# Two projections of a hybrid attention block as groups of seven block products inside the last attention heads

## The chip, the cores and the metric

The kernel runs on one core of a Trainium2 chip. Times are microseconds (us) of device time of one execution. TensorE is PE, VectorE DVE, ScalarE ACT, GpSimd POOL, SyncE SP (here it only issues transfers).

## The reference, cut to what matters

```
h = rms_norm(x, norm_g)                       # x: 512 tokens x 1024, float32
proj = h @ w_in                               # 1024 x 6152
fq,fk,fv,fz, mq,mk,mv,mz, ga,gb, fl = split(proj)   # 8 x 512, 2 x 1024, 8 columns
y_fox  = fox_attention(rms(fq), rms(fk), fv, log_sigmoid(fl + b_f)) * silu(fz)
y_moba = moba_attention(rope(rms(mq)), rope(rms(mk)), mv) * silu(mz)
merged = sigmoid(ga + b0) * (y_fox @ w_fox) + sigmoid(gb + b1) * (y_moba @ w_moba)
out = x + merged @ w_out
```

Each branch has 8 heads of 64. With 512 tokens and key blocks of 256, both attentions are causal attention over 512 keys.

## The kernel before, in words

Every float32 product is made of three float32r products. `split` makes of a weight chunk (128 x 1024) a rounded part `wh` (ACT, L134) and a rest `wl` (DVE, L136); the activations are held as `Gh` and `Gl`; PE adds Gh·wh + Gh·wl + Gl·wh.

A plain projection of 256 columns (`mkb` is k of the last four MoBA heads, `mqb` their q, `mvb` their v) is 4 `unit`s of 128 tokens, each 2 x 4 x 3 matmuls of 256 columns: 96 matmuls. A group (`GZ0` is z of MoBA, both halves; `GA0`, `GA1`, `GB0`, `GB1` are the gates) computes a 2 x 2 block product with seven block products instead of eight. It needs differences of the weight blocks (DVE, `sub`) and sums of the activations, which are made early, written to DRAM (`s_dram`) and read back (`load_sums`, by POOL's queue, when the stage `gates` begins). One of the seven products is 24 matmuls of 256 columns.

Four attention stages (`plan`) of four heads each: fox a, fox b, MoBA a, MoBA b. For each pair of heads `Tr` transposes q and k (`p_qT`, `p_kT`) and writes `QS`, `KH`, `KL`; a transfer copies `KH` to the other half of the partitions. For each head `Aa` makes four logit tiles (`lg`, PE), each masked with its row maximum taken (DVE, tile `p` and `negm`, L558) and exponentiated (ACT); `Bb` transposes the probabilities (`p_a`, `p_b`, `p_cc`), splits them (`pth` on ACT, `ptl` on DVE) and multiplies by v (`pv`); the result `y` (`yma`, `ymb`) is one DVE addition, and RECIPROCAL takes the inverse row sums of a pair of heads. The transposes rotate through three PSUM tiles (`tp`).

`inter` puts work from a list (`filler`) between the steps of a stage: in MoBA a `mkb`, `mqb` and half of `mvb`, in MoBA b the rest of `mvb` and `wf0` to `wf3` (y_fox @ w_fox, 24 matmuls of 512 columns each, tile `pf`). Then come `GZ0`, `GA0` and the rest. `pump` issues loads of weight chunks (SP's queue, four buffers `wr`) and their splits up to three places ahead of the unit that is reached; with `issue_after` the splits of `wf` stand behind the last DVE instruction written so far. A scheduler then fixes the order on every engine at build time; the engines run it in that order.

Of the kernel before, what the change touches and what calls it, by code (L numbers as in the profile page):

```python
# [29 lines left out]
def fox_moba_kernel(ctx: ExitStack, tc, xT, x, w_in, w_fl, w_fox, w_moba, w_out, cst, rope, out):  # L30
# [203 lines left out]
    rbc = con.tile([P, S], F32, name="rbc")  # L234


    def norm_row():
# [450 lines left out]


    PRODUCTS = (("A11", 1), ("S3", 3), ("A12", 2), ("S2", 1), ("S1", 1), ("A22", 3), ("S4", 1))  # L690
    Z_ORDER = (0, 2, 1, 3, 5, 4, 6)
    groups = {}

    def group(name):
        ga, gz, i = name[1] == "A", name[1] == "Z", int(name[2])
        wa, wb = ("mza", "mzb") if gz else (f"g{'a' if ga else 'b'}{i}", f"g{'a' if ga else 'b'}{i + 2}")
# [12 lines left out]

        def prep(n):  # L710

            def go():
                if n == 1:
                    sub(R["11"], R["12"], R["11"])
                    sub(R["12"], R["22"], R["12"])
                elif n == 3:
                    sub(R["12"], R["22"], R["11"])
                elif n == 5:
                    sub(R["21"], R["21"], R["12"])
                key = ("11", "12", "21", "12", "11", "21", "22")[n]  # L720
# [32 lines left out]
        def add(u, half, n, b):  # L753
            V.tensor_tensor(out=u[:, :, half * HT:(half + 1) * HT], in0=two(st[b]), in1=two(st["e", n]), op=OP.add)

        def evac(n):
            if n == 0:
                if ga or i == 0 and not gz:
# [20 lines left out]
        def silu2(o, z):  # L779
            s = t2("u", 3, "sg").rearrange("p (c t) -> p c t", t=z.shape[2])  # L780
            A.activation(s, z, AF.Tanh, scale=0.5)
            V.scalar_tensor_tensor(o, s, 1.0, z, op0=OP.add, op1=OP.mult)

        def finish_z(q):
            u = st["u"][q]
            for c in range(2):
                o = u[:, :, c * HT:(c + 1) * HT] if q else u[:, c:c + 1, :]
                silu2(o, two(st[1]) if q and c == 0 else o)
            for c in range(2):
                G.tensor_tensor(out=YM[2 * q + c], in0=YM[2 * q + c], in1=u[:, c, :], op=OP.mult)  # L790

        def finish(q):
            if gz:
                return finish_z(q)
# [19 lines left out]
        groups[name] = [unit(n) for n in order_]  # L814

    def merge_a(i, c):
        if True:
# [53 lines left out]
    def group_o():  # L871
# [94 lines left out]
        def evac(n):  # L966
# [13 lines left out]
            else:  # L980
# [260 lines left out]
```

## Time and profile before

| | |
|---|---|
| three timed runs | 424.75, 424.85, 425.29 us (median 424.85) |
| the profiled execution | 424.55 us, its span 422.8 us |
| granted TensorE clock, mean | 0.998 |
| busy, share of the span | PE 98%, DVE 79%, ACT 65%, POOL 26% |

The span is the time from the first to the last record; all times below count from its start. The profiled execution lies 0.3 us under the median of the timed runs.

### The profile page before, as it was taken

Reading aid. Unit: us, or ns where it says so; the run is one execution under the profiler, and the core shown is the slowest. Engines: PE = TensorE matmul, PEld = TensorE weight load, DVE = VectorE, ACT = ScalarE, POOL = GpSimd, SP = SyncE. Lnnn points to the kernel's source line nnn. Section 1 sums busy time; section 2 is a strip of 40 time slices with the busy share of each in tenths; the row PEclk is TensorE's granted clock in tenths of the full one; section 3 lists DMA queues with packets and bytes.
Section 4 is the critical chain, followed back from the end, with each engine's and each line's share of the span. In section 5 each row is a group of like instructions: output and inputs, shape, how many; then the busy total and the mean of one; then the engine's idle time right before and its main releaser. Section 6 shows DMA issues by size and latency. Waiting matters only on the chain.

```text
span 422.8 us, 7826 instructions
## 1 busy us (share of the span) xinstructions
PE 415.2 (98%) x2956; PEld 387.7 (92%) x2956; DVE 334.5 (79%) x571; ACT 273.6 (65%) x521; POOL 109.5 (26%) x127
## 2 busy tenths in 40 slices
PE   7999999999999999999999999999999999999996
PEld 6998899999999999999988789999999989988884
DVE  4669978798889877597457769998998675788982
ACT  4985337877788767797379845666756525685550
POOL 1059300252023880417501042134000020022240
PEclk9999999999999999999999999999999999999999
DMA  7981244654264432241211039705151726796494
GB/s 246 399 314 50 60 140 137 183 165 154 50 226 120 158 101 80 71 121 32 99 34 44 28 96 373 252 13 188 39 162 52 248 51 152 243 246 108 82 159 159
DMA packets 26373, 59.52 MB, mean 141 GB/s; under 512 B 3168, under 2 KB 7968, under 8 KB 26336
## 3 DMA queue, kind: packets, MB, share of 16 engines
q1 hardware_dynamic: 13552, 38.38, 27.5%
q0 software_dynamic: 3968, 9.44, 10.4%
q10 hardware_dynamic: 8816, 11.21, 9.1%
q8 instruction: 23, 0.38, 0.4%
q14 instruction: 14, 0.11, 0.1%
HBM read 48.37 MB, written 6.32 MB: 129 GB/s over the span
## 4 chain that ended last, share of the span: by engine, by line
PE 83%; DVE 6%; DMA 5%; ACT 2%; issue 2%; SPq 1%; DVEq 0%; ACTq 0%
PE pb_GB L744 3%; PE pb_GA L744 3%; PE pb_GA L741 3%; PE pb_GB L741 3%; PE pb_GA L743 3%; PE pb_GB L743 3%; PE po L943 3%; PE po L945 3%; PE po L944 3%; PE pv L609 2%; PE pv L610 2%; PE lg L556 2%; PE lg L555 2%; PE pf L666 2%; PE pf L668 2%; DMA x<-in_x_dram 2%
## 5 line engine op out<-in xcount | busy, mean ns | idle before, releaser
L330 POOL TENSOR_TENSOR ff<-ss,mh 128x8 f32<-128x8 f32 x16 | 28.3, 1771 | 59.4 <-DVE ss L328 58.8
L560 ACT ACTIVATE p<-p,negm 128x128 f32<-128x128 f32 (+1 forms) x64 | 35.6, 557 | 8.9 <-DVE negm L558 8.6
L558 DVE CUSTOM_DVE_ANT_0 p<-lg,mask 128x128 f32<-128x128 f32 (+1 forms) x64 | 30.2, 485 | 8.3 <-PE lg L556 6.9
L134 ACT ACTIVATE wh_GB<-wr_gb 128x1024 fp32r<-128x1024 f32 x14 | 14.6, 1058 | 13.9 <-PE pm L667 5.9
L905 ACT ACTIVATE wh_o<-wr_o 128x1024 fp32r<-128x1024 f32 x14 | 14.8, 1060 | 9.7 <-PE pb_GB L743 2.8
L555 PE MATMUL lg<-KH,QS 128*128 128x128 f32 (+1 forms) x64 | 20.9, 332 | 0.0
L136 DVE TENSOR_TENSOR wl_GB<-wr_gb,wh_GB 128x1024 fp32r<-128x1024 f32 x14 | 16.8, 1220 | 5.0 <-ACT wh_GB L134 5.0
L136 DVE TENSOR_TENSOR wl_GA<-wr_ga,wh_GA 128x1024 fp32r<-128x1024 f32 x14 | 19.2, 1388 | 1.5 <-ACT wh_GA L134 1.5
L906 DVE TENSOR_TENSOR wl_o<-wr_o,wh_o 128x1024 fp32r<-128x1024 f32 x14 | 16.9, 1220 | 2.4 <-ACT wh_o L905 2.3
L134 ACT ACTIVATE wh_GA<-wr_ga 128x1024 fp32r<-128x1024 f32 x14 | 14.4, 1056 | 6.9 <-DVE wr_ga L702 3.0
L826 POOL DMA_DIRECT2D uGB<-f x4 | 3.5, 871 | 58.2 <-issue 48.2
L529 DVE SCALAR_TENSOR_TENSOR QS<-p_qT,cs,QS 64x512 fp32r<-64x512 f32 x16 | 12.0, 750 | 5.7 <-ACT QS L528 5.4
L606 DVE TENSOR_TENSOR ptl<-p_b,pth 128x512 fp32r<-128x512 f32 x16 | 11.0, 684 | 6.2 <-ACT pth L605 6.1
L528 ACT ACTIVATE QS<-p_qT,cs 64x512 fp32r<-64x512 f32 x16 | 10.9, 681 | 4.4 <-PE p_qT L519 3.0
L744 PE MATMUL pb_GA<-Gh,wl_GA 128*128 128x256 f32 x48 | 13.5, 281 | 0.0
L744 PE MATMUL pb_GB<-Gh,wl_GB 128*128 128x256 f32 x48 | 13.5, 281 | 0.0
L743 PE MATMUL pb_GA<-Gl,wh_GA 128*128 128x256 f32 x48 | 13.5, 281 | 0.0
L741 PE MATMUL pb_GA<-Gh,wh_GA 128*128 128x256 f32 x48 | 13.5, 281 | 0.0
L741 PE MATMUL pb_GB<-Gh,wh_GB 128*128 128x256 f32 x48 | 13.5, 280 | 0.0
L743 PE MATMUL pb_GB<-Gl,wh_GB 128*128 128x256 f32 x48 | 13.5, 280 | 0.0
L666 PE MATMUL pf<-yhf,wh_wf 128*128 128x512 f32 x32 | 13.0, 407 | 0.3 <-ACT f L680 0.3
L668 PE MATMUL pf<-yhf,wl_wf 128*128 128x512 f32 x32 | 12.6, 403 | 0.2 <-DVE wl_wf L136 0.2
(483 smaller groups left out, 1821.4 us busy)
## 6 DMA issues: line engine op xcount, KB each, us to landing
wr_ga<-in_w_in_dram SPq DMA_DIRECT2D x8, 512.0 KB
wr_gb<-in_w_in_dram SPq DMA_DIRECT2D x8, 512.0 KB
wr_o<-in_w_out_dram SPq DMA_DIRECT2D x8, 512.0 KB
xt<-in_xT_dram SPq DMA_DIRECT2D x8, 256.0 KB
x<-in_x_dram SPq DMA_DIRECT2D x8, 256.0 KB
KH<-KH ACTq DMA_DIRECT2D x16, 128.0 KB
s_dramh<-sum_h ACTq DMA_DIRECT2D x8, 256.0 KB
s_draml<-xt ACTq DMA_DIRECT2D x8, 256.0 KB
```

The lines of the kernel that those rows point to most:

```text
L134: A.activation(hi[:, :, 0:n], src, AF.Copy)
L136: eng.tensor_tensor(out=lo[:, q, 0:n], in0=src[:, q], in1=hi[:, q, 0:n].bitcast(F32), op=OP.subtract)
L330: G.tensor_tensor(out=f2, in0=ss.rearrange("p t h -> p (t h)"), in1=mh, op=OP.pow)
L555: T.matmul(lg[:, :n], qs[:, qt], kh[:, :n], start=True, stop=False)
L558: V.tensor_tensor_reduce(pt, lg[:, :n], mask[:, 512 - n:512], -0.125, 3.0e38, op0=OP.add, op1=OP.min, accum_out=mkn[:, hh, i:i + 1])
L560: A.activation(pt, pt, AF.Exp, bias=mkn[:, hh, i:i + 1], scale=-1.0, accum_out=rs[:, hh, i:i + 1])
L666: T.matmul(p, hi[:, k, cc], yh, start=(k == 0), stop=False)
L668: T.matmul(p, lo[:, k, cc], yh, start=False, stop=(k == 3))
L741: T.matmul(o, hi[:, k, cc], lh, start=(n < 3 and c == 0 and k == 0), stop=False, skip_group_check=True)
L743: T.matmul(o, hi[:, k, cc], ll, start=False, stop=False, skip_group_check=True)
L744: T.matmul(o, lo[:, k, cc], lh, start=False, stop=(k == 3), skip_group_check=True)
L906: V.tensor_tensor(out=wide(lo), in0=wide(R[key, c]), in1=wide(hi).bitcast(F32), op=OP.subtract)
```

## The change

`mqb` and `mkb` become one group `GQ0` of seven products (q and k side by side as two weight columns, tokens as rows): 168 matmuls in place of 192. `GZ0` moves from behind the attention into the filler of MoBA b, ahead of `wf0`; `wf1` to `wf3` move behind the attention. Both groups read their sums through small slots: `A` is the two fox tiles `Q2t` and two `sm` tiles, `B` the tile of `rbc` and three `y` tiles, `C` the second token half of `Gh` and `Gl` (free once `mvb` is done). Each slot is loaded twice by SP's queue. `load_sums` stays for the gates.

```diff
-            ("m", "a", C_MQ, C_MK, ["mkb", "mqb", "mvb:01"]),
-            ("m", "b", C_MQ, C_MK, ["mvb:23", "wf0", "wf1", "wf2", "wf3"]))
+            ("m", "a", C_MQ, C_MK, ["GQ0", "mvb:01"]),
+            ("m", "b", C_MQ, C_MK, ["mvb:23", "GZ0", "wf0"]))
...
-                def go(i=first_prep[nm] + ahead(nm, n), u=u, late=nm[:2] == "wf"):
+                def go(i=first_prep[nm] + ahead(nm, n), u=u, late=nm in ("GZ0", "wf0")):
...
     load_sums()
-    for n, u in enumerate(filler(["GZ0"])):
-        u()
-        if n == 1:
-            gate[0]()
+    gate[0]()
+    groups["gate", "GZ0"](1)
+    seq(["wf1", "wf2", "wf3"])
     seq(["GA0"])
...
+    Z_ORDER = (0, 1, 3, 5, 4, 2, 6)
+    Q_ORDER = (0, 2, 3, 1, 4, 5, 6)
...
+    def sums_load(slot, what):
+        for d, pair in zip(S_dram, slot):
+            for i, t in enumerate(pair):
+                nc.sync.dma_start(out=t.bitcast(F32), in_=d[S_AT[what], :, 2 * i:2 * i + 2, :])
+        SLOT[what] = slot
...
+        def prep(n):
+            def go():
+                if n == 1:
+                    sub("11", "12", "11")
+                    sub("12", "22", "12")
+                elif n == 3:
+                    sub("12", "22", "11")
+                elif n == 5:
+                    sub("12", "21", "12")
+                B[n] = split(R[("11", "12", "21", "12", "11", "12", "22")[n]], CW, f"{name}{n}")
+            return go
...
+            def go():
+                if n == order_[0]:
+                    for i, kind in enumerate(kinds):
+                        slots[i] = sums_slot(name, kind)
+                        sums_load(slots[i], PRODUCTS[sums[i]][0])
+                product(n)
+                evac(n)
+                if n in sums[:2]:
+                    i = sums.index(n)
+                    sums_load(slots[i], PRODUCTS[sums[i + 2]][0])
+            return go
```

Three places show what the scheduler made of it. On DVE, before, behind the RECIPROCAL of the first pair of MoBA b (names ending in a number are tiles; `p_...` is a tile of masked logits):

```order
L529 SCALAR_TENSOR_TENSOR QS<-p_qT,cs,QS 64x512
L533 SCALAR_TENSOR_TENSOR KL_858<-p_kT,cs,KH 64x512
L575 RECIPROCAL rinv<-rsum 128x8
L558 ISA p_3321,negm<-lg,mask 128x128
```

With the change, at the same RECIPROCAL:

```order
L532 SCALAR_TENSOR_TENSOR QS<-p_qT,cs,QS 64x512
L578 RECIPROCAL rinv<-rsum 128x8
L729 TENSOR_TENSOR wr_mzb_2680<-wr_mzb_2744,wr_mza_2578 128x1024
L536 SCALAR_TENSOR_TENSOR KL_857<-p_kT,cs,KH 64x512
L638 TENSOR_TENSOR yma_3022<-pv,ysh 64x512
L532 SCALAR_TENSOR_TENSOR QS<-p_qT,cs,QS 64x512
L609 TENSOR_TENSOR ptl<-p_a,pth 128x512
L136 TENSOR_TENSOR wl_GZ_3210<-wr_mzb_2680,wh_GZ_3209 128x4x256
L561 ISA p_3397,negm<-lg,mask 128x128
L561 ISA negm 128x1
L536 SCALAR_TENSOR_TENSOR KL_858<-p_kT,cs,KH 64x512
```

The weight of the third product of `GZ0` (its difference and its split `wl_GZ_3210`) now stands here. On PE, before, at the first logits of the third head of MoBA b:

```order
L667 MATMUL pf_3345<-ylf_2118,wh_wf_3116 128x512
L668 MATMUL pf_3345<-yhf_2117,wl_wf_3117 128x512
L666 MATMUL pf_3345<-yhf_2481,wh_wf_3116 128x512
L555 MATMUL lg<-KH,QS 128x128
L556 MATMUL lg<-KL_857,QS 128x128
L609 MATMUL pv<-pth,v_mvb 128x512
```

With the change:

```order
L602 MATMUL p_a<-ident,p_3119 128x128
L558 MATMUL lg<-KH,QS 128x128
L559 MATMUL lg<-KL_857,QS 128x128
L558 MATMUL lg<-KH,QS 128x256
L559 MATMUL lg<-KL_857,QS 128x256
L612 MATMUL pv<-pth,v_mvb 128x512
L771 MATMUL pGZ0a_3228<-Gh,wh_GZ_3209 128x256
L602 MATMUL p_b<-ident,p_3107 128x128
L602 MATMUL p_b<-ident,p_3113 128x128
L602 MATMUL p_b<-ident,p_3119 128x128 x2
L602 MATMUL p_cc<-ident,p_3113 128x128
L602 MATMUL p_cc<-ident,p_3119 128x128
```

No projection stands between attention rows here until `pGZ0a`; counted back from it, 53 attention rows of PE (from the first logits of MoBA b on) have none among them. On SP's queue, with the change, inside `GQ0` (before, `wr_mvb` was followed by the loads of `wf`):

```order
L210 DMA wr_mvb_2504<-in_w_in_dram 128x1024
L210 DMA wr_mvb_2576<-in_w_in_dram 128x1024
L712 DMA Q_853<-s_dramh 128x512
L712 DMA GQ_a_2453<-s_draml 128x512
L712 DMA Q_854<-s_dramh 128x512
L712 DMA GQ_a_2454<-s_draml 128x512
L736 DMA wr_mza_2578<-in_w_in_dram 128x1024
```

The second filling of slot A (`Q`, `GQ_a`) stands behind the two loads of `mvb`.

## Rows read from the trace of the kernel before

**Rows 1.** Stretches: us; busy PE, PEld, DVE, ACT, POOL (instructions); clock, DMA share, GB/s.

```profile
143.35:214.87 71.52, 71.52 (x583) 70.45 (x582) 50.46 (x107) 48.86 (x110) 32.81 (x43) 1.00 0.30 91
214.87:256.12 41.25, 40.34 (x223) 33.23 (x221) 28.97 (x65) 30.04 (x72) 6.48 (x7) 1.00 0.25 68
256.12:277.82 21.70, 21.70 (x183) 21.62 (x182) 20.79 (x22) 13.80 (x18) 5.49 (x6) 1.00 0.74 272
```

**Rows 2.** PE by line, 214.87 to 256.12: count, busy us, mean ns, idle us before.

```profile
L666 PE MATMUL pf<-yhf,wh_wf 128*128 128x512 f32 x32 | 13.0, 407 | 0.3 <-ACT f L680 0.3
...
L555 PE MATMUL lg<-KH,QS 128*128 128x128 f32 (+3 forms) x16 | 5.5, 353 | 0.0
...
L609 PE MATMUL pv<-pth,v_mvb 128*128 128x512 f32 (+3 forms) x12 | 4.0, 344 | 0.4 <-DVE ymb L635 0.4
...
L599 PE MATMUL p_b<-ident,p 128*128 128x128 f32 x20 | 3.1, 272 | 0.0
```

**Rows 3.** Timeline of PE: start, us, instruction; 30 matmuls of GZ0 in a row.

```profile
257.25 0.28 PE L741 MATMUL pb_GZ<-Gh,wh_GZ 128*128 128x256 f32 x1
...
260.67 0.28 PE L744 MATMUL pb_GZ<-Gh,wl_GZ 128*128 128x256 f32 x1
```

**Rows 4.** Timeline of PE, attention in MoBA b.

```profile
217.91 0.31 PE L555 MATMUL lg<-KH,QS 128*128 128x128 f32 x1
...
223.59 0.60 PE L519 MATMUL p_qT<-ident,qn_mqb 128*128 128x128 f32 x4
223.95 0.42 PE L609 MATMUL pv<-pth,v_mva 128*128 128x384 f32 x1
224.21 0.34 PE L610 MATMUL pv<-ptl,v_mva 128*128 128x384 f32 x1
```

**Rows 5.** Timeline of DVE, logits of the first pair of MoBA b; idle time in brackets.

```profile
218.36 0.29 DVE L558 CUSTOM_DVE_ANT_0 p<-lg,mask 128x128 f32<-128x128 f32 x1 [0.47 <-PE lg L556]
...
225.75 0.29 DVE L558 CUSTOM_DVE_ANT_0 p<-lg,mask 128x128 f32<-128x128 f32 x1
...
225.97 0.42 DVE L558 CUSTOM_DVE_ANT_0 p<-lg,mask 128x256 f32<-128x256 f32 x1
...
226.31 0.74 DVE L533 SCALAR_TENSOR_TENSOR KL<-p_kT,cs,KH 64x512 fp32r<-64x512 f32 x1
...
232.06 0.20 DVE L575 RECIPROCAL rinv<-rsum 128x8 f32<-128x8 f32 x1 [0.47 <-ACT p L560]
```

**Rows 6.** Timeline of DVE without gaps, second pair of MoBA b.

```profile
239.78 0.55 DVE L558 CUSTOM_DVE_ANT_0 p<-lg,mask 128x384 f32<-128x384 f32 x1
...
240.25 0.68 DVE L635 TENSOR_TENSOR ymb<-pv,ysh 64x512 f32<-64x512 f32 x1
240.86 1.21 DVE L136 TENSOR_TENSOR wl_wf<-wr_wf,wh_wf 128x1024 fp32r<-128x1024 f32 x1
241.99 0.68 DVE L558 CUSTOM_DVE_ANT_0 p<-lg,mask 128x512 f32<-128x512 f32 x1
...
242.60 0.68 DVE L606 TENSOR_TENSOR ptl<-p_b,pth 128x512 fp32r<-128x512 f32 x1
243.20 0.41 DVE L606 TENSOR_TENSOR ptl<-p_cc,pth 128x256 fp32r<-128x256 f32 x1
243.53 0.68 DVE L606 TENSOR_TENSOR ptl<-p_a,pth 128x512 fp32r<-128x512 f32 x1
```

**Rows 7.** Timeline of DVE, a weight difference of GZ0 and what follows.

```profile
256.60 1.23 DVE L702 TENSOR_TENSOR wr_mzb<-wr_mzb,wr_mzb 128x1024 f32<-128x1024 f32 x1
257.75 0.68 DVE L606 TENSOR_TENSOR ptl<-p_b,pth 128x512 fp32r<-128x512 f32 x1
```

**Rows 8.** Timelines of DVE and POOL where both work.

```profile
250.34 3.45 DVE L136 TENSOR_TENSOR wl_GZ<-wr_mza,wh_GZ 128x1024 fp32r<-128x1024 f32 x2
...
228.32 1.30 POOL L651 TENSOR_TENSOR yma<-yma,rinv_bc 128x512 f32<-128x512 f32 x1 [19.14 <-DVE yma L635]
249.24 2.33 POOL L651 TENSOR_TENSOR ymb<-ymb,rinv_bc 128x512 f32<-128x512 f32 x1 [19.62 <-DVE ymb L635]
```

More of the change, by code (lines that the diff above doesn't have):

```diff
@@ L193, in stream @@
         first_prep[name] = len(preps)
+        if name in ("GQ0", "GZ0"):
+            group_2(name)
+            return
         if name[0] == "G":
@@ L232, in x_stats @@
         G.tensor_tensor(out=r, in0=mm, in1=mh[:, :NT], op=OP.pow)
-    rbc = con.tile([P, S], F32, name="rbc")
+    rbc = sb.tile([P, S], F32, name="rbc", tag="row", bufs=1)
     def norm_row():
@@ L690, in fox_moba_kernel, with sums_slot @@
     PRODUCTS = (("A11", 1), ("S3", 3), ("A12", 2), ("S2", 1), ("S1", 1), ("A22", 3), ("S4", 1))
-    Z_ORDER = (0, 2, 1, 3, 5, 4, 6)
     groups = {}
+    SLOT = {}
+    Z_ORDER = (0, 1, 3, 5, 4, 2, 6)
+    Q_ORDER = (0, 2, 3, 1, 4, 5, 6)
+    def sums_slot(name, kind):
+        if kind == "A":
+            tiles = [(Q2t[0], Q2t[1]), tuple(t2("sm", 2, f"{name}_a{i}", dt=F32R) for i in range(2))]
+        elif kind == "B":
+            tiles = [(t2("row", 1, "slot_b3", dt=F32R), t2("y", 13, "slot_b0", dt=F32R)),
+                     tuple(t2("y", 13, f"slot_b{i}", dt=F32R) for i in (1, 2))]
+        else:
+            return [[x[:, 2 * i:2 * i + 2, HT:S] for i in range(2)] for x in (Gh, Gl)]
+        return [[t.rearrange("p (k t) -> p k t", t=HT) for t in pair] for pair in tiles]
@@ new lines, in sums_load, with left_2, group_2, sub @@
+    def sums_load(slot, what):
[3 more added lines that the diff above has]
+        SLOT[what] = slot
+    def left_2(what, k):
+        if what[0] == "S":
+            return [pair[k // 2][:, k % 2] for pair in SLOT[what]]
+        return left(what, k)
+    def group_2(name):
+        gq = name == "GQ0"
+        first, second = ("mkb", "mqb") if gq else ("mza", "mzb")
+        order_ = Q_ORDER if gq else Z_ORDER
+        porder = (0, 2, 1, 3, 4, 5, 6) if gq else order_
+        st, R, B, slots = {}, {}, {}, {}
+        base = len(preps)
+        def sub(o, a, b):
+            V.tensor_tensor(out=R[o], in0=R[a], in1=R[b], op=OP.subtract)
+        def load(key):
+            nm, hf = (first, second)[key[1] == "2"], int(key[0]) - 1
+            def go():
+                R[key] = sb.tile([P, 4, CW], F32, name=f"wr_{nm}{hf}", tag="wr", bufs=WR)
+                nc.sync.dma_start(out=R[key], in_=w_in[COLS[nm] // CW, :, 4 * hf:4 * hf + 4, :])
+            return go
[10 more added lines that the diff above has]
+            return go
+        for key in ("11", "21", "12", "22") if gq else ("11", "12", "22", "21"):
+            last = max(porder.index(n) for n in {"11": (0, 4), "12": (1, 3, 5), "21": (2, 5), "22": (6, 1, 3)}[key])
+            loads.append((load(key), base + last))
+        preps.extend(prep(n) for n in porder)
+        def product(n):
+            what = PRODUCTS[n][0]
+            b = {0: "a", 1: "b", 3: "a", 5: "b", 4: "a", 2: "b", 6: "a"}[n]
+            new = n < 3
+            if new:
+                st[b] = pj(f"p{name}{b}{n}")
+            p = st[b]
+            hi, lo = B[n]
+            for h in range(2):
+                o = p[:, h * CW:(h + 1) * CW]
+                c = slice(h * P, (h + 1) * P)
+                for k in range(4):
+                    lh, ll = left_2(what, k)
+                    wh, wl = hi[:, k, 0:CW], lo[:, k, 0:CW]
+                    for i, (a, w) in enumerate(((lh, wh), (lh, wl), (ll, wh))):
+                        x, y = (a[:, c], w) if gq else (w[:, c], a)
+                        T.matmul(o, x, y, start=(new and h == 0 and k == 0 and i == 0), stop=(k == 3 and i == 2),
+                                 skip_group_check=True)
+        def two(b):
+            return st[b].rearrange("p (a b) -> p a b", a=2)
+        def at(q, half):
+            if gq:
+                nm = (first, second)[q]
+                if nm not in QN:
+                    QN[nm] = sb.tile([P, NT, CW], F32, name=f"qn_{nm}", tag="qk", bufs=4)
+                return QN[nm][:, 2 * half:2 * half + 2, :]
+            if ("u", q) not in st:
+                st["u", q] = sb.tile([P, 2, S], F32, name=f"u{name}{q}", tag="qk", bufs=4)
+            return st["u", q][:, :, half * HT:(half + 1) * HT]
+        def keep(q, half, b):
+            A.activation(at(q, half), two(b), AF.Copy)
+        def add(q, half, b):
+            o = at(q, half)
+            V.tensor_tensor(out=o, in0=two(b), in1=o, op=OP.add)
+        def ready(q, half):
+            nm, ts = (first, second)[q], slice(2 * half, 2 * half + 2)
+            norm_qk(nm, ts)
+            do_rope(nm, ts)
+        def silu2(o, z):
+            s = t2("u", 3, "sg").rearrange("p (c t) -> p c t", t=z.shape[2])
+            A.activation(s, z, AF.Tanh, scale=0.5)
+            V.scalar_tensor_tensor(o, s, 1.0, z, op0=OP.add, op1=OP.mult)
+        def gate_y(q):
+            for c in range(2):
+                G.tensor_tensor(out=YM[2 * q + c], in0=YM[2 * q + c], in1=st["u", q][:, c, :], op=OP.mult)
+        def evac(n):
+            if n == 0:
+                keep(0, 0, "a")
+            elif n == 1:
+                keep(1, 1, "b")
+            elif n == 3:
+                keep(0, 1, "a")
+            elif n == 5:
+                add(0, 1, "b")
+                if gq:
+                    ready(0, 1)
+            elif n == 4:
+                add(1, 1, "a")
+                if gq:
+                    ready(1, 1)
+                else:
+                    silu2(at(1, 1), at(1, 1))
+            elif n == 2:
+                add(0, 0, "b")
+                if gq:
+                    ready(0, 0)
+                else:
+                    for c in range(2):
+                        z = st["u", 0][:, c:c + 1, :]
+                        silu2(z, z)
+                    gate_y(0)
+            elif gq:
+                keep(1, 0, "a")
+                ready(1, 0)
+            else:
+                silu2(at(1, 0), two("a"))
+        def unit(n):
+            sums = [m for m in order_ if PRODUCTS[m][0][0] == "S"]
+            kinds = "AB" if gq else "AC"
+            def go():
+                if n == order_[0]:
[7 more added lines that the diff above has]
+                    sums_load(slots[i], PRODUCTS[sums[i + 2]][0])
+            return go
+        groups[name] = [unit(n) for n in order_]
+        groups["gate", name] = gate_y
@@ L694, in group @@
     def group(name):
-        ga, gz, i = name[1] == "A", name[1] == "Z", int(name[2])
-        wa, wb = ("mza", "mzb") if gz else (f"g{'a' if ga else 'b'}{i}", f"g{'a' if ga else 'b'}{i + 2}")
+        ga, i = name[1] == "A", int(name[2])
+        wa, wb = f"g{'a' if ga else 'b'}{i}", f"g{'a' if ga else 'b'}{i + 2}"
         st = {}
@@ L757, in evac @@
             if n == 0:
-                if ga or i == 0 and not gz:
+                if ga or i == 0:
                     u = [sb.tile([P, 2, S], F32, name=f"u{name}{q}", tag="qk", bufs=4) for q in range(2)]
@@ L777, in evac @@
                 finish(1)
[L779 to L790, printed above, removed]
         def finish(q):
-            if gz:
-                return finish_z(q)
             u, j0 = st["u"][q], 2 * i + 4 * q
@@ L813, in unit @@
             return go
-        groups[name] = [unit(n) for n in order_]
+        groups[name] = [unit(n) for n in range(7)]
     def merge_a(i, c):
@@ L986, in group_o @@
         groups["WO"] = late_loads
-    order = ["fqa", "fka", "fza", "fzb", "fva", "fkb", "fqb", "fvb", "mka", "mqa", "mva", "mkb", "mqb", "mvb", "wf0", "wf1", "wf2", "wf3",
-             "GZ0", "GA0", "GA1", "GB0", "wm0", "wm2",
+    order = ["fqa", "fka", "fza", "fzb", "fva", "fkb", "fqb", "fvb", "mka", "mqa", "mva", "GQ0", "mvb", "GZ0", "wf0", "wf1", "wf2", "wf3",
+             "GA0", "GA1", "GB0", "wm0", "wm2",
              "GB1", "wm1", "wm3", "WO"]
```

7 lines of the change are left out of this document (3 added, 4 removed).

## The prediction

> **What bounds the kernel now.** I read the busy times by stretch first. From 143.35 to 277.82 us PE is busy 133.56 of 134.47 us at the full granted clock, 1.00, while DVE has room: 50.46 of 71.52 us up to the end of `mvb`, 28.97 of 41.25 us in MoBA b [rows 1]. (PE's rows are the same in both kernels up to `mkb`.) So PE bounds the kernel, and a row taken off PE is worth its full pitch, if DVE keeps up. Next, PE's lines in MoBA b: they wait by name 0.3 us for `f` and 0.4 us for `ymb` [rows 2], and hardly for anything else. The busy time hides some more, since a modelled end covers a short wait; for that I took pitches (start to start) from the timeline. Thirty matmuls of 256 columns in a row go from 257.25 to 260.67 us: 29 steps in 3.42 us, **0.118 us each** [rows 3]. I scale this with the columns: 0.235 us for 512, 0.177 for 384, 0.06 for 128. A transpose takes 0.09 (four in 0.36), and the first matmul behind transposes some 0.08 more (0.26 for 384 columns in place of 0.177) [rows 4]. With these, the 41.25 us from 214.87 us on, in which `wf` is the filler, hold 96 matmuls of 512 columns in three lines like the first shown (22.6 us), 32 logits of 128 to 512 columns (4.7, with 0.4 for those behind transposes 5.1), 33 `pv` (5.2 by the same count) and 59 transposes (5.3) [rows 2]: 38.2 us. So about 3 us there are not PE's own work; some 2% is what such pitches may be off. I take **2.3 us of waits inside MoBA b** today.
>
> DVE's pitches, from stretches in which it has no gap: a masked logit tile 0.22, 0.34, 0.47 or 0.61 us for 128 to 512 columns, 1.64 us a head [rows 5, 6]; `ptl` 0.60 (512 columns) or 0.33 (256), `y` 0.61, a split 1.13 [rows 6]; `QS` and `KL` some 0.75 each, RECIPROCAL 0.2 [rows 5]; a weight difference 1.15 [rows 7].
>
> **The change, part by part.**
>
> *PE's work.* `mkb` and `mqb` were 2 x 96 matmuls of 256 columns; `GQ0` is 168. Nothing else on PE gets fewer or more: 24 x 0.118 = **-2.85 us** [rows 3]. That `GZ0` and `wf1` to `wf3` change places costs PE nothing by itself.
>
> *DVE inside `GQ0`.* Plain projections split four chunks, the group seven: 3 x 1.13 = 3.4 us; four differences, 4 x 1.15 = 4.6; three additions out of PSUM, 3 x 0.61 = 1.8: 9.8 us. And the first two weights of `GZ0` are now made here, two differences and two splits: 4.6 us. From 143.35 to 214.87 us DVE was busy 50.5 us of 71.5 [rows 1]; now about 64.9 of 71.5 - 2.85 = 68.7. Only 3.8 us are left, in a stretch in which DVE also serves two pairs of heads. PE's waits here can be nothing (the splits run three places ahead) or as much as the slack that is left, some 4 us; from rows that show 94% busy against 71% now, I take **+1.0 us**.
>
> *The last heads, and the place of the third weight.* This is the step that decides. The splits of `GZ0` are written "behind the last DVE instruction so far", and the difference and split of its third weight land behind the RECIPROCAL of the first pair of MoBA b (the order of DVE above). Its product `pGZ0a` therefore cannot start earlier. Before, `pf` matmuls stood between the attention rows; now there are 53 attention rows of PE, from the first logits of MoBA b on, with nothing among them. What PE has from there to the row that needs `wl_GZ_3210`: 20 logits (2 x 1.18 + 0.36 = 2.7 us), 16 `pv` (2.35), 31 transposes (2.8), some nine steps from transposes to matmuls (0.7), one matmul of `GZ0` (0.1): **8.6 us** [rows 3, 4]. What DVE has to do in the same time, in its order, from the first masked tile on, up to the `KL` of the second pair (which frees the PSUM tile that `p_cc` waits for): two heads of tiles and one more tile, 3.5 us; four `ptl` of 512 and two of 256 columns, 3.1; two `y`, 1.2; two `QS` and two `KL`, 3.0; RECIPROCAL 0.2; the difference 1.15; the split 1.13. That is 13.3 us [rows 5 to 7]. Ahead of it are 0.45 us from the first logit to the first tile (217.91 to 218.36 us), and behind it 0.5 us of transposes and `pv` until the matmul [rows 4, 5]: 14.25 us against 8.6. So PE must wait at least **14.25 - 8.6 = 5.7 us**, even if DVE never stops. The upper end is from the same stretch today: from the first tile to RECIPROCAL DVE takes 232.06 - 218.36 = 13.70 us [rows 5], while its rows up to there now add up to 7.3, since it waits in turn for logits, exponentials and `pv`. With that pace it is 5.7 + 6.4 = 12.1 us. Today's 13.70 us are stretched mostly by PE, which has `pf` to do in between and is in no hurry for logits; without `pf` PE answers at once, so I stay near the lower end: 5.7 + 1.3 for the chain from logit through tile and exponential to transpose, **+7.0 us**.
>
> *Waits that go.* Of the 2.3 us of waits in MoBA b some were for `ymb` and `f` [rows 2]; `wf1` to `wf3` behind the attention are long matmuls with everything ready, and they cover the last `y`. I take **-2.0 us**, between 0 and -2.3.
>
> *Transfers.* The sums read through the slots cost no engine but SP time, and the chip's transfers are slack here: 91 and 68 GB/s, against 272 GB/s in 256.12 to 277.82 us [rows 1]. I cost them at nothing; the cover is work on PE of other products, and one place of it is thin (a rival below).
>
> *Sum.* -2.85 + 1.0 + 7.0 - 2.0 = +3.15 us. The profiled execution took 424.55 us, so it would take 427.7; that execution is 0.3 under the median of the timed runs, so the median becomes **428.0 us**, slower by 0.7%.
>
> **A rule against this change.** When two wide splits of `GZ0` were made while POOL multiplied `ymb`, DVE needed 3.45 us for the two, and POOL 2.33 us for a product that takes 1.30 us otherwise; one split alone is 1.21 us [rows 6, 8]. The two thus cost each other about 1 us. The Trainium skill, page "SBUF — State Buffer", section "Who interferes with whom", says that a DVE instruction with two inputs in SBUF and a GpSimd instruction that reads SBUF shut each other out, and the later one waits. By that rule the trace agrees, with its 1.03 us on either side; and the rule speaks against a group here, because it is rich in such DVE rows.
>
> **Rivals.**
>
> *A: the last heads are covered after all (other side).* If DVE runs its 13.3 us without a gap, PE's wait is the 5.7 us of the floor; if the slack of 3.8 us holds in `GQ0` (nothing in place of 1.0), and all of today's waits around these heads go (the 2.3 us, and up to 1.2 us that the error of my count may hide), the sum is -2.85 - 3.5 + 5.7 = -0.65: 424.2 us. It is the size of one wait that decides: with the other terms so, the kernel is faster by over 0.2% once that wait is below 5.5 us. For it: RECIPROCAL and the difference might run earlier than their place in my sum if the scheduler's order is kinder than a serial reading, and part of the waiting PE time can lie ahead of the first logits. Against it: the 13.3 us are a sum of pitches that no row undercuts.
>
> *B: sums that come late.* The second filling of slot A is 1 MB on SP's queue behind two loads of `mvb`, another 1 MB (the order of SP above). At 272 GB/s [rows 1] a MB takes 3.9 us, both 7.7. The cover is the last product of slot B, 24 x 0.118 = 2.8 us, and about 1.3 us of attention: 4.1. PE could wait 3.6 us more: 431.6 us. Against it: the loads of `mvb` may have been issued long before the slot is free, and then only 3.9 us stand against 4.1.
>
> *C: DVE and POOL block each other in `GQ0`.* There are now 11 wide DVE rows with two inputs (seven splits and four differences) in place of four, and POOL is busy 32.81 of 71.52 us there [rows 1], so about 0.46 of the time. Seven more rows x 0.46 x 1.03 us = 3.3 us of DVE time, most of the 3.8 that are left; with half of that seen by PE, +1.6: 429.6 us. Against it: POOL's rows were there before too, and the order may keep them apart.
>
> *D: the change does nothing.* The rows do move and 24 fewer matmuls are certain; no change is to be had only where costs cancel, which A covers.
>
> **How the numbers follow.** My forecast has 0.58; A 0.22; B 0.12; C 0.08. About 0.85 us, 0.2%, is what a measurement of this kernel can tell from no change: faster is below 424.0, slower above 425.7. My likeliest case has its own range of 425.4 to 431.5: the wait in the last heads from 5.7 to 10.5 us with the other terms as taken, and one of them at its end. A's centre is 424.2, so it is split: 0.13 faster, 0.09 same. The forecast's lower edge gives another 0.03 faster and 0.08 same; B and C are slower. Faster 0.16, same 0.17, slower 0.67. The range for 8 in 10 leaves out the lower half of A and the far end of B and of the wait: 423.6 to 431.8 us.
>
> **What would show it.** In the trace after: PE without work for 5 to 8 us in all between the first logits of MoBA b and the matmul that needs `wl_GZ_3210`, with DVE's rows (`p`, `ptl`, `KL`, the difference, the split) as what ended the waits; DVE above 90% busy in that stretch and in `GQ0`; 24 PE matmuls fewer; `wf1` to `wf3` behind the attention in one piece without waits. If PE's wait lies in front of a product of `GQ0` and a transfer ends it, B was right; if `wl_GQ` takes 1.7 us in place of 1.13 where POOL works, C was. I would be wrong first if PE's wait in the last heads is under 5 us: then DVE had been further ahead than the order lets me see, or its rows are shorter than their pitches of today.

## The result and the profile after

The changed kernel takes 431.04 us (median of four runs, 430.46 to 432.06) against 425.07 us: ratio 1.014, 95% interval 1.0122 to 1.0158. It is slower by 6.0 us, where 3.15 us was forecast. Four more runs of it, told below, gave 430.52 us and 1.0125 (1.011 to 1.014). The profiled execution is the slowest of the first four (432.06 us, span 430.4 us), so the sizes below are a little above the median's. Of its 7.5 us over the profile of before, 0.9 are lost ahead of 131 us, where no row was changed.

PE ran 2932 instructions in place of 2956, so the 24 matmuls are gone. What PE waited for, in the list of waits of the kernel after (total us, times, longest; compare [rows 2]):

```profile
PE lg L558 <- DMA KH<-KH: 4.1, 2, 3.7
PE p_qT L522 <- POOL qn_mqa L371: 2.4, 1, 2.4
...
PE pv L612 <- DVE yma L638: 0.8, 1, 0.8
```

The busy times by stretch (columns as in [rows 1]), cut where `GQ0` begins (167.06), where the first logits of MoBA b begin (221.15), on both sides of the longest wait, and where the clock is back:

```profile
143.35:167.06 23.71, 21.36 (x175) 20.89 (x174) 18.51 (x33) 13.41 (x30) 17.79 (x21) 1.00 0.43 134
167.06:215.00 47.94, 47.54 (x386) 46.57 (x385) 42.78 (x87) 35.91 (x77) 21.10 (x26) 1.00 0.54 176
...
221.15:229.96 8.81, 7.73 (x53) 6.39 (x51) 6.68 (x22) 6.82 (x22) 0.00 (x0) 1.00 0.52 155
229.96:234.21 4.25, 0.60 (x7) 0.39 (x5) 3.59 (x6) 4.15 (x10) 0.16 (x1) 0.89 0.14 31
234.21:240.10 5.89, 5.89 (x26) 5.70 (x26) 5.79 (x11) 4.04 (x9) 1.12 (x1) 0.50 0.11 25
240.10:262.00 21.90, 21.90 (x167) 21.08 (x167) 18.48 (x31) 15.70 (x30) 3.68 (x3) 1.00 0.67 204
```

Three things are to be seen. PE loses 2.35 us ahead of `GQ0`, in the first row. It does almost nothing for 4.25 us among the last heads. And behind that hole it is busy without a gap for 5.89 us at a granted clock of 0.50, the lower of its two levels (1.2 GHz). The timeline of PE shows what that means: two matmuls of 256 columns in a row of `GZ0` stand 0.22 us apart at first, and 0.12 us once the clock is back.

```profile
229.96 0.60 PE L602 MATMUL p_a<-ident,p 128*128 128x128 f32 x4
234.21 0.45 PE L558 MATMUL lg<-KH,QS 128*128 128x128 f32 x1 [3.65 <-DMA KH<-KH]
...
239.25 0.41 PE L771 MATMUL pGZ0a<-Gh,wh_GZ 128*128 128x256 f32 x1
239.47 0.41 PE L771 MATMUL pGZ0a<-Gh,wl_GZ 128*128 128x256 f32 x1
...
240.33 0.28 PE L771 MATMUL pGZ0a<-Gh,wh_GZ 128*128 128x256 f32 x1
240.45 0.28 PE L771 MATMUL pGZ0a<-Gh,wl_GZ 128*128 128x256 f32 x1
```

By pitches, the work of those 5.89 us takes 3.05 us at full clock: the low clock costs 2.8 us, nearly as much as the wait ahead of it. What the wait was for is seen on ACT's timeline: `KH` of the second pair stands behind the exponentials of the second head, and PE goes on 2.3 us after its transfer is issued at 231.87 us.

```profile
230.46 0.71 ACT L563 ACTIVATE p<-p,negm 128x512 f32<-128x512 f32 x1
...
231.16 0.67 ACT L534 ACTIVATE KH<-p_kT,cs 64x512 fp32r<-64x512 f32 x1
...
231.87 0.48 ACTq L535 DMA_DIRECT2D KH<-KH  x1
```

ACT itself was late there. It writes the inverse row sums (4 KB) to DRAM and reads them back, and in its order the issue of the read waits for the write; `ysh`, which the next `y` needs, stands behind it:

```profile
222.80 0.27 ACTq L586 DMA_DIRECT2D r_dram<-rinv_t  x1
...
225.81 0.47 ACTq L592 DMA_DIRECT2D rinv_bc<-r_dram  x1
226.33 0.59 ACT L637 ACTIVATE ysh<-pv 64x512 f32<-64x512 f32 x1 [1.79 <-PE lg L559]
```

The same two issues in the kernel before:

```profile
219.00 0.27 ACTq L583 DMA_DIRECT2D r_dram<-rinv_t  x1
...
220.26 1.12 ACTq L589 DMA_DIRECT2D rinv_bc<-r_dram  x2
```

They lie 3.01 us apart in place of 1.26, and ACT stands still for 1.79 us. (The profile names PE's logits as what ended that; by the semaphores of the trace the write landed at 225.64 us, just ahead of the issue.) The DMA engines were busy 0.72 of the time between the two issues, 0.02 before: SP had issued a filling of slot A, 1 MB, from 219.61 us on. That this filling held up the write is read from these numbers, not tried.

The other loss is POOL's. Its timeline where it scales and turns the first half of `qn_mqa`, in the kernel before:

```profile
147.45 2.03 POOL L332 TENSOR_TENSOR qn_mqa<-qn_mqa,ff 128x512 f32<-128x512 f32 x1
149.56 0.46 POOL L362 TENSOR_TENSOR ra<-qn_mqa,tab_mq 128x128 f32<-128x128 f32 x1
149.98 1.30 POOL L364 TENSOR_TENSOR rb<-qn_mqa,tab_mq 128x64 f32<-128x64 f32 x1
151.25 0.32 POOL L366 TENSOR_TENSOR rb<-qn_mqa,tab_mq 128x64 f32<-128x64 f32 x1
151.64 0.47 POOL L368 TENSOR_TENSOR qn_mqa<-ra,rb 128x128 f32<-128x128 f32 x1
```

In the kernel after:

```profile
150.00 2.02 POOL L335 TENSOR_TENSOR qn_mqa<-qn_mqa,ff 128x512 f32<-128x512 f32 x1
152.10 1.33 POOL L365 TENSOR_TENSOR ra<-qn_mqa,tab_mq 128x128 f32<-128x128 f32 x1
153.38 1.30 POOL L367 TENSOR_TENSOR rb<-qn_mqa,tab_mq 128x64 f32<-128x64 f32 x1
154.65 0.31 POOL L369 TENSOR_TENSOR rb<-qn_mqa,tab_mq 128x64 f32<-128x64 f32 x1
155.04 1.51 POOL L371 TENSOR_TENSOR qn_mqa<-ra,rb 128x128 f32<-128x128 f32 x1
```

And DVE's in the same time:

```profile
151.59 1.51 DVE L729 TENSOR_TENSOR wr_mkb<-wr_mqb,wr_mkb 128x1024 f32<-128x1024 f32 x1
153.03 1.48 DVE L136 TENSOR_TENSOR wl_GQ<-wr_mkb,wh_GQ 128x1024 fp32r<-128x1024 f32 x1
...
155.03 1.21 DVE L729 TENSOR_TENSOR wr_mqb<-wr_mqb,wr_mqb 128x1024 f32<-128x1024 f32 x1
```

Two more of the five POOL rows take 1.3 to 1.5 us in place of 0.5, just where a wide DVE row of `GQ0` runs; the five take 6.55 us from first start to last end in place of 4.66. POOL also begins them 2.55 us later than before (150.00 against 147.45 us; by 0.9 PE is late too), which uses up the 1 us that they had to spare (152.11 against 153.08 us, when PE took them).

### The profile page after: what moved, and what is told of

The parts are those of the page before. It is cut to its first block, busy times and chain, and to the rows that moved or that the text cites. A ratio compares the mean times of both kernels' runs of the same rounds, so it can differ in the third digit from the quotient of the medians.

```text
span 430.4 us, 7858 instructions
## 1 busy us (share of the span) xinstructions
PE 415.6 (97%) x2932; PEld 388.0 (90%) x2932; DVE 343.6 (80%) x581; ACT 275.2 (64%) x520; POOL 111.3 (26%) x127
## 4 chain that ended last, share of the span: by engine, by line
PE 71%; DVE 10%; DMA 8%; ACT 5%; issue 2%; POOL 2%; SPq 1%; ACTq 1%; DVEq 0%; POOLq 0%
PE pb_GA L907 3%; PE pb_GB L907 3%; PE pb_GA L906 3%; PE pb_GB L904 3%; PE pb_GA L904 3%; PE pb_GB L906 3%; PE po L1092 3%; PE po L1093 3%; PE po L1091 3%; PE pGZ0a L771 3%; DMA x<-in_x_dram 2%; PE pGQ0b L771 2%; PE pGZ0b L771 2%; PE pGQ0a L771 2%; PE pm L670 2%
## 5 line engine op out<-in xcount | busy, mean ns | idle before, releaser
L136 DVE TENSOR_TENSOR wl_GA<-wr_ga,wh_GA 128x1024 fp32r<-128x1024 f32 x14 | 17.0, 1222 | 10.1 <-ACT wh_GA L134 10.1
L136 DVE TENSOR_TENSOR wl_GB<-wr_gb,wh_GB 128x1024 fp32r<-128x1024 f32 x14 | 16.8, 1220 | 5.0 <-ACT wh_GB L134 5.0
L558 PEld LDWEIGHTS lg<-KH,QS 128*128 128x128 f32 x64 | 12.2, 193 | 4.5 <-ACT pth L608 3.9
L637 ACT ACTIVATE ysh<-pv 64x512 f32<-64x512 f32 x16 | 9.5, 593 | 7.8 <-PE pv L613 3.5
```

What stands on the lines that cost most here:

```text
L136: eng.tensor_tensor(out=lo[:, q, 0:n], in0=src[:, q], in1=hi[:, q, 0:n].bitcast(F32), op=OP.subtract)
L558: T.matmul(lg[:, :n], qs[:, qt], kh[:, :n], start=True, stop=False)
```

## The experiments

**z put back behind the attention, `GQ0` kept.** The edit: the filler of MoBA b and the group behind it are those of before.

```diff
-            ("m", "b", C_MQ, C_MK, ["mvb:23", "GZ0", "wf0"]))
+            ("m", "b", C_MQ, C_MK, ["mvb:23", "wf0", "wf1", "wf2", "wf3"]))
```

> GQ0 in MoBA a as in the change, but z behind the attention as before and wf0 to wf3 in MoBA b. Theory 1 (the loss sits in MoBA b: third weight of GZ0 behind RECIPROCAL, no filler on PE, and PE's clock halved behind the stall): the 8.8 us lost between 215 and 240 us go, the 2.1 us of waits of before come back, 431.0 - 8.8 + 2.1 = 424.3 us, with GQ0's own waits (qn_mqa about 2.5, GQ0 about 1.2) still in it. Theory 2 (GQ0's load on DVE delays everything, the last heads too): 429 us or more.

431.41 us (429.2 to 433.81), ratio 1.0146 (1.0101 to 1.019). Theory 1 alone falls: `GQ0` by itself costs as much as the whole change. The wait for `qn_mqa` is there (2.4 us), and with `wf` as filler in MoBA b PE waits 1.4 us for `f` and 1.0 for `yma`. By pitches, MoBA b loses about 3 us more than before, though its rows and their order are those of before. The profiled execution (433.81 us) is the slowest of the four, and 2.8 us of it are lost ahead of 131 us and some 2 in front of `GA0`, where nothing was changed; so the size of this run is uncertain by more than those of the others.

**Only z moved.** `mkb` and `mqb` plain again, the rest as changed.

```diff
-            ("m", "a", C_MQ, C_MK, ["GQ0", "mvb:01"]),
+            ("m", "a", C_MQ, C_MK, ["mkb", "mqb", "mvb:01"]),
```

> mkb and mqb as plain projections as before, GZ0 and wf0 in MoBA b and wf1 to wf3 behind as in the change. Theory 1: the stall of the last heads and the halved clock are there without GQ0: 425.1 + 8.8 - 2.1 = 431.8 us, less what DVE is earlier (its first two weights may be made sooner): 429 to 432. Theory 2: 423 to 425.

427.94 us (427.5 to 428.86), ratio 1.0066 (1.0043 to 1.0088). Slower than before without `GQ0`, but short of 429: no single hole and no low clock (mean 1.00), but waits of up to 0.9 us between 227 and 236 us. Of the profiled execution's 3.7 us over before, 1.4 are lost in the first 20 us, where nothing was changed, and 2.4 in MoBA b. The order is not that of the change with `GQ0` taken out: the third weight of `GZ0` stands behind the same RECIPROCAL (at 233.54 us), but products of `GZ0` stand among the first head's logits. So it does not show what the tie alone costs in the order of the change.

**z's weights free.** One word: the difference and the splits of `GZ0` are no longer tied behind the last DVE row.

```diff
-                def go(..., late=nm in ("GZ0", "wf0")):
+                def go(..., late=nm == "wf0"):
```

> The change with one word different: the weights of GZ0 are no longer tied behind the last DVE instruction, only wf0's are, so that products of GZ0 stand between the attention rows from the first logits of MoBA b on. Theory 1: wait and clock go, 431.0 - 8.8 = 422.2 us, up to 424 with new small waits. Rival (the wait named by the profile, for the transfer of KH behind four exponentials on ACT, is ACT's and not DVE's): the third pair of logits is as late as before, but PE has work; no lower than 428 if PE still ends up behind KH.

426.88 us (424.93 to 430.51, ten runs), ratio 1.0058 (1.0027 to 1.0088). The hole is gone: the list names no wait of PE between 215 and 275 us, and PE is busy 60.00 of 60.00 us. So the wait for `KH` was no bound; it showed only because PE had nothing else. But the time falls less than expected, and its runs are far apart.

**Idle matmuls in the hole.**

```diff
+                if br + half == "mb" and h == 2:
+                    junk = pst("lg", 2, "junk")
+                    for i in range(14):
+                        T.matmul(junk, qs[:, 0:P], qs, start=True, stop=True)
```

> The change, with 14 idle matmuls of 512 columns (their result is thrown away) ahead of the third head's logits of MoBA b, in the hole in which PE waits 3.7 us. They add about 3.3 us of PE work there and take nothing out of the wait. If the halved clock behind the hole costs its 2.8 us: 431.0 - 2.8 = 428.2 us. Rival (DVE is behind at that place, and PE would have waited for it at full clock too): 430.5 to 431.5 us, with named waits of PE for DVE in place of slow matmuls.

429.28 us (429.03 to 431.53), ratio 1.0106 (1.0075 to 1.0137): 1.8 us under the changed kernel's first four runs, 1.2 under the four later. More work on PE, and a shorter time. PE's timeline at that place:

```profile
231.47 3.47 PE L557 MATMUL junk<-QS 128*128 128x512 f32 x14 [0.24 <-DVE QS L532]
234.88 0.30 PE L562 MATMUL lg<-KH,QS 128*128 128x128 f32 x1
```

The matmuls take 0.23 us each and end at 234.9 us, 2.3 us behind the issue of `KH`'s transfer (232.55), where PE went on in the changed kernel too, so they fill the hole and no more; the granted clock stays 1.00 from 226 to 242 us. That is what the low clock costs in the end, shown by itself, and it is below the 2.8 us worked out: at full clock PE loses by pitches 1.4 us more to waits behind the hole (0.4 and 0.6 of it in front of two `pv`), so half of the clock's price stood in for waits. The profiled execution (431.53 us) is the longest of the four: behind its wait of 2.2 us for `qn_mqa` the clock is 0.62 from 155.6 to 160 us.

**`GQ0`'s first differences held back.** The differences and splits that the first product's step issues are put behind `v_mva`'s second tile.

```diff
+                    if nm == "GQ0" and n == 0:
+                        with tc.issue_after(ANCHOR[0]):
+                            pump(i)
...
+                    if nm == "mva" and n == 1:
+                        ANCHOR.append(last_on(mybir.EngineType.DVE))
```

> The change, with the first two weight differences of GQ0 and the splits behind them held on DVE until v_mva's second tile, so that they no longer run while POOL normalises and turns the first half of qn_mqa. Theory 3 (wide two-input DVE rows slow POOL's rows, and PE waits 2.4 us for qn_mqa): that wait falls to about 0.3 us as before, and the time by up to 2.4: 428.6 us. Rival (POOL is late because the rows ahead of it on DVE are more, not because they meet): the wait stays at 1.5 us or more, 430 to 431 us.

429.51 us (428.09 to 430.09), ratio 1.009 (1.0057 to 1.0124); the wait for `qn_mqa` falls from 2.4 to 0.3 us, and the time by 1 to 1.5. POOL's timeline at the same rows:

```profile
151.63 1.33 POOL L365 TENSOR_TENSOR ra<-qn_mqa,tab_mq 128x128 f32<-128x128 f32 x1
152.91 0.33 POOL L367 TENSOR_TENSOR rb<-qn_mqa,tab_mq 128x64 f32<-128x64 f32 x1
153.19 0.33 POOL L369 TENSOR_TENSOR rb<-qn_mqa,tab_mq 128x64 f32<-128x64 f32 x1
153.60 0.46 POOL L371 TENSOR_TENSOR qn_mqa<-ra,rb 128x128 f32<-128x128 f32 x1
```

**Both repairs,** the held differences and the free weights of z.

> Both repairs: GZ0's weights free (as in the run that freed them) and the first differences of GQ0 held back. If both are sound and independent, 426.9 - 1.2 to 426.9 - 2.4: 424.5 to 425.7 us, as fast as before. If GQ0's load on DVE is what decides, holding rows back only moves the waits into GQ0: 426.5 to 428 us.

422.27 us (421.91 to 423.53), ratio 0.9933 (0.9911 to 0.9954): faster than either kernel, and below the range expected of it. The list of waits of this kernel has, besides the start of the program, no more than

```profile
PE p_qT L522 <- POOL qn_mqb L371: 0.8, 1, 0.8
PE pf L669 <- ACT f L683: 0.5, 1, 0.5
PE p_qT L522 <- POOL qn_mqa L371: 0.3, 1, 0.3
PE lg L558 <- DMA KH<-KH: 0.3, 1, 0.3
```

and in its stretches DVE is as full as expected of the change (47.02 of 49.81 us), with PE hardly stopping:

```profile
165.19:215.00 49.81, 48.74 (x395) 47.70 (x393) 47.02 (x88) 37.21 (x79) 24.11 (x26) 1.00 0.52 167
215.00:240.00 25.00, 25.00 (x203) 24.54 (x204) 20.67 (x37) 19.46 (x38) 0.00 (x0) 1.00 0.71 229
```

**The kernel before with the group's load on DVE.**

```diff
+                for _ in range(2 if name in ("mkb", "mqb") else 0):
+                    V.tensor_tensor(out=lo[:, :, 0:CW], in0=raw[0], in1=hi[:, :, 0:CW].bitcast(F32), op=OP.subtract)
```

> The kernel before, each of the four splits of mkb and mqb made three times on DVE (the same result again): eight more wide two-input rows, 9.2 us, about what GQ0 adds, and PE's work as before. Theory 2 (the load on DVE in MoBA a is the cost): PE's wait for qn_mqa comes up to 2 us, waits of 1 to 2 us inside mkb and mqb and 2 to 3 us in MoBA b: 429 to 432 us. Rival (DVE has room, as the busy share of 71% says; the cost of GQ0 is its own dependencies: sums, differences, additions): 425 to 426 us.

429.59 us (428.88 to 430.1), ratio 1.0098 (1.0073 to 1.0122): 4.0 us from eight DVE rows, PE's work untouched. The list of waits:

```profile
PE pf L669 <- ACT f L683: 1.9, 1, 1.9
...
PE p_qT L522 <- POOL qn_mqa L371: 1.1, 1, 1.1
PE pv L612 <- DVE ymb L638: 0.7, 2, 0.4
PE pf L671 <- DVE wl_wf L136: 0.6, 1, 0.6
```

Inside `mkb` and `mqb` PE waits for nothing. What is lost beyond `qn_mqa` is lost in MoBA b, 4 to 5 us more than before by pitches, and it includes a stretch of low clock (mean 0.90 from 218 to 235 us). So the room that DVE's busy share promised was no room for these rows: the loss comes in the next stage. How it gets there (later heads, and ACT behind them, which is what `f` waited for) is argued from the waits, not shown.

**Only z moved, its weights free.** The edits of the second and the third experiment together.

> mkb and mqb plain as before, GZ0 in MoBA b with its weights free, wf1 to wf3 behind. Theory 1 (the place of GZ0's weights makes the stall; wf behind covers the last heads): no waits beyond those of before up to 215 us, and the 2.1 us of before's waits in MoBA b gone: 425.0 - 2.1 = 423 us. Theory 2 alone (only GQ0's load matters) says the same; if GZ0 inside the heads costs by itself, 426 to 428 as with its weights tied.

424.54 us (422.73 to 425.62, ten runs), ratio 0.9978 (0.9961 to 0.9994). A gain of 0.2%, less than expected: from 20 to 215 us nothing is lost (0.6 us ahead of that), and in MoBA b by pitches about 2.4 us, hardly less than the 2.1 to 2.9 of before.

**Repeats.** The kernel with both repairs, and the changed kernel, with more rounds.

> The kernel with both repairs once more, to size it against the kernel before: 421.9 to 423.5 us as in the first runs, ratio 0.993. If the first result was luck of a few executions: 424 us or more.

422.24 us (421.5 to 423.06, six runs), ratio 0.993 (0.9915 to 0.9946).

> The changed kernel itself once more, for a second profile and more runs. If the steps found in its first trace are its own: 430.5 to 431.5 us, with PE's waits for qn_mqa (2.4 us) and for KH (3.7 us) and the low clock behind them again; the 1 us lost ahead of 131 us may go, since no row there was changed.

430.52 us (430.29 to 430.87), ratio 1.0125 (1.011 to 1.014). In the second profile (430.29 us) 0.2 us are lost ahead of 131 us, the wait for `qn_mqa` is 1.2 us, that for `KH` 3.6 with 3 to 4 us of low clock behind it (1.7 us lost by pitches), and PE waits 0.7 us for the sums of slot A.

**DVE rows with one input.**

```diff
+        for _ in range(3 if name[:3] in ("mkb", "mqb") else 0):
+            V.tensor_scalar(lo[:, :, 0:n], src, 1.0, None, op0=OP.mult)
```

> The kernel before with three more wide DVE rows ahead of each of the four splits of mkb and mqb, that read one tile and not two (twelve rows, their result is overwritten by the split). Theory 3 (it takes two inputs in SBUF to slow POOL): POOL's rows for qn_mqa keep their 0.3 to 0.5 us while such a row runs, PE waits no more for qn_mqa than before (0.3 us), and what is lost in MoBA b goes with the time that the rows take on DVE: about 4 us if they take 10 us in all, 1 to 2 us if 5. Rival (any wide DVE row slows POOL): rows of POOL of 1.3 us in place of 0.3, and a wait of over 1 us for qn_mqa.

426.09 us (425.28 to 426.89, ten runs), ratio 1.0019 (1.0008 to 1.003). Theory 3 in its narrow form falls. The rows are short (0.68 us alone; some 10 us in all, with what POOL adds), and yet they and POOL's rows stretch each other. POOL's rows for `qn_mqa`:

```profile
151.44 0.79 POOL L364 TENSOR_TENSOR ra<-qn_mqa,tab_mq 128x128 f32<-128x128 f32 x1
152.20 1.30 POOL L366 TENSOR_TENSOR rb<-qn_mqa,tab_mq 128x64 f32<-128x64 f32 x1
153.46 0.77 POOL L368 TENSOR_TENSOR rb<-qn_mqa,tab_mq 128x64 f32<-128x64 f32 x1
```

DVE's in the same time (L136 has one input, L138 is the plain split, with two):

```profile
147.17 4.74 DVE L136 TENSOR_SCALAR wl_mkb<-wr_mkb 128x1024 fp32r<-128x1024 f32 x4
...
152.05 1.27 DVE L138 TENSOR_TENSOR wl_mkb<-wr_mkb,wh_mkb 128x1024 fp32r<-128x1024 f32 x1
153.24 0.81 DVE L136 TENSOR_SCALAR wl_mkb<-wr_mkb 128x1024 fp32r<-128x1024 f32 x1
```

The POOL row of 1.30 us stands beside the plain split, as one of 1.30 us did before. Beside one-input rows stand those of 0.79 and 0.77 us (0.46 and 0.32 alone), and four one-input rows take 4.74 us in place of 2.7. So one input is enough to stretch both sides. PE waits 1.2 us for `qn_mqa`, as with two inputs. In MoBA b, though, next to nothing is lost, with as much DVE time added as in the run with two inputs: what the heads pay depends on where the rows fall, and I can't derive it from their sum.

**z's weights free, once more.**

> The change with GZ0's weights free once more: its runs lay between 424.9 and 430.5 us, and the profiled one was the fastest. If the slow ones come from a stall somewhere with the low clock behind it, a second profile should show a place where PE waits over 2 us and the clock is 0.5 for some us; if they come from the stretch ahead of 131 us, waits there.

429.07 us (425.65 to 430.64), ratio 1.0071 (1.0035 to 1.0106). The second profile is of one of the longer executions (429.68 us): PE waits 2.3 us for `qn_mqa` where the first had 1.0, and this time the clock falls behind that wait:

```profile
156.00:158.00 2.00, 1.25 (x7) 1.25 (x7) 1.94 (x5) 0.26 (x1) 1.15 (x2) 0.62 0.95 341
158.00:160.00 2.00, 2.00 (x12) 2.00 (x11) 1.43 (x6) 1.16 (x4) 1.52 (x1) 0.52 0.06 22
```

Both profiles also have 1.9 to 2.0 us of PE waiting for `wh_GB` past 307 us, which is not there with both repairs; I did not follow it up.

## Why the prediction was wrong, and where it was right

The direction and the place of the hole held; its reason held by half, and the size did not. 3.15 us were forecast and 5.3 to 6.0 measured, inside the range.

- **PE bounds the kernel:** held. Every us lost is PE waiting or PE at half clock.
- **PE's work, -2.85:** held; 24 instructions fewer.
- **DVE inside `GQ0`, +1.0:** near. DVE was busy 18.51 + 42.78 = 61.3 us up to 215 us (64.9 forecast); by pitches PE loses 0.8 us more inside than before in the first profile and 1.9 in the second, 0.7 of it for slot A. DVE was 89% busy there (42.78 of 47.94 us), where over 90% was the sign.
- **The last heads, +7.0:** near in size, half right in its reason. From the first logit at 221.15 us to the matmul that needs `wl_GZ_3210` at 237.55 us pass 16.4 us with 8.6 us of PE's work; of the 7.8 us between, 1.6 belong to the low clock (half of 237.55 - 234.21), which leaves 6.2 us of waits, just above the floor of 5.7. But that the floor was met is partly luck: DVE was not busy without a gap, as the floor assumes, but 6.68 + 3.59 of 13.06 us (79%). Heads, exponentials, `KH` and its transfer were waited for in turn, ACT being the full engine in the hole (4.15 of 4.25 us), after it had stood for 1.79 us for a transfer. The forecast of DVE rows as what ends the waits failed for the longest, which a transfer ended. With PE given other work (z's weights free) the chain costs nothing, so the hole needs the tied weights; with `mkb` and `mqb` plain they made no such hole, so it needs this order as well. (60 attention rows stand ahead of `pGZ0a` in the trace, counted one by one, not 53; the prediction's own count for its sum fits.)
- **Waits that go, -2.0:** not shown by itself. From 240.10 us PE is busy throughout in the changed kernel, but today's waits, some 3 us by pitches, lie mostly among the same heads as the new ones; and in the run with only z moved and its weights free 2.4 us stay.
- **Transfers, 0:** wrong, though rival B's 3.6 us didn't come. PE waited 0.7 us for slot A in the second profile, none in the first. But in both profiles the two issues of ACT shown above lie 3.0 us apart in place of 1.3, which held up ACT in the chain of the last heads. What of PE's wait this made was not tried.
- **The step that failed** is the sum itself, which had no term for two things. The first is `qn_mqa`: 1.2 to 2.4 us of PE waiting ahead of `GQ0`, because POOL begins its rows later and they are stretched by the group's first differences and splits. Rival C named that meeting, but I gave it 0.08, counted it as DVE's lost time inside `GQ0`, and overlooked that the scheduler had put these rows before the group begins, beside the POOL rows that PE waits for. C's sign did come there: the group's first rows on DVE take 2.08, 1.51 and 1.48 us; from 166 us on its rows take 1.21 to 1.23, with no meeting. The run that only moved the first differences gave 1 to 1.5 us back. The second is PE's clock behind the hole: 2.8 us by pitches in the first profile and 1.7 in the second, 1.2 to 1.8 by the run that kept PE busy there. I had priced a wait as a wait.

What the profiles of the changed kernel lose more than the one of before, by pitches (start to start, against the same kinds of rows at full clock):

| | forecast | first profile | second |
|---|---|---|---|
| PE's work | -2.85 | -2.85 | -2.85 |
| up to 131 us | 0 | 0.9 | 0.2 |
| 131 us to `GQ0` | 0 | 2.6 | 1.5 |
| inside `GQ0`, to the end of `mvb` | 1.0 | 0.8 | 1.9 |
| MoBA b without the low clock | 7.0 - 2.0 | 3.5 | 3.5 |
| low clock in MoBA b | 0 | 2.8 | 1.7 |
| sum | 3.15 | 7.75 | 5.95 |
| measured (less 424.55) | | 7.51 | 5.74 |

So MoBA b as a whole came near its forecast by luck: its waits were priced 1.5 us too high, and the clock, which was not in the sum, made up for it. What is over in the total is mostly the wait for `qn_mqa`. (The lower edge of the likeliest case, 425.4 us, takes more than one term at its end: 428.0 - 1.3 - 1.0 is 425.7. It decided nothing.)

My account of the two halves as independent was wrong too: `GQ0` alone costs 6.4 us and z alone 2.9, both together 6.0. DVE rows with two inputs added in MoBA a are paid in MoBA b as well: by pitches `GQ0` alone loses 3.4 us more there than before, and the kernel before with that load 4.5. With z's free products, work that waits for no head, MoBA b loses no more than before. Both repairs together give over 8 us, where one alone gave 1 to 1.5 (the held differences) and 1.5 to 4 (the free weights). The two profiles with free weights alone show where theirs stays: they lose 1.2 and 3.9 us more than before between 131 us and `GQ0`, the larger with the low clock behind the wait for `qn_mqa`, and both 2.4 us at `wh_GB`; with both repairs it is 0.2 to 0.6, and nothing at `wh_GB`. Why the one-input rows cost MoBA b nothing, and why `wh_GB` is late, stays open.

## What to carry to other kernels

A group of fewer block products moves work from PE to the engine that makes its differences; count that engine's rows not only where the group runs but where the scheduler pulls them, and see which small rows of POOL stand beside them. Before a filler's weights are tied behind a row of a chain, look whether the filler is what keeps PE busy during that chain: here freeing them and moving two differences turned a loss of 1.4% into a gain of 0.7%. A hole of some 4 us on PE should be priced with the slow matmuls behind it, not with its own length alone; here that was 1.7 to 2.8 us more. And where a chain passes through DRAM, look which large transfers run beside it: here a small write took 3.0 us in place of 1.3 beside one of 1 MB.

## What the runs showed of the hardware

- Behind PE's wait of 3.65 us the granted clock was 0.50 for 5.89 us of busy PE. Behind a wait of 2.35 us it stayed at 1.00 in one execution (the first profile, 157 us) and fell to 0.52 in another (158 to 160 us in the last run, behind 2.3 us): beside the same rows of two kernels, two prices. This is one reason why runs of these kernels lie up to 5.6 us apart, where those of before stay within some 2: of the first ten runs with z's weights free, the three longest (429.5 to 430.5 us) have a mean clock of 0.990, the others 0.994 to 1.000.
- POOL's short rows were stretched by DVE rows with one input as well: 0.46 to 0.79 us and 0.32 to 0.77, while the DVE rows went from 0.68 to as much as 1.71 us. The Trainium skill, page "SBUF — State Buffer", section "Who interferes with whom", says that `tensor_scalar` in a two-port mode also takes the pair of ports that DVE shares with GpSimd. The rows agree: they take 0.68 us where a row with two inputs and as many elements takes 1.2, and they and POOL's rows lengthen each other.
- ACT's issue of a read that needs a 4 KB write to DRAM came 1.26 us behind the write's issue with the DMA engines 2% busy, and 3.01 us behind it with them 72% busy; ACT's next row stood behind it.
